# Second norm of a hybrid decoder layer: weight product formed ahead of the row factor, residual added in one operation per half

## Chip, cores, metric

The kernel runs on one core of a Trainium2 chip. The metric is the device time of one execution in microseconds; the times given are medians over runs. A profile is one execution taken by the hardware profiler; its times count from the start of its span.

## What is computed

One layer of a decoder trunk for 512 tokens of width 1024, in float32. The input is normalised and projected; eight heads of block-sparse attention and four heads of a matrix memory make the two halves of `mixed`; then come the output projection, a norm with the residual, and an MLP. The change lies between the output projection and the MLP:

```python
def rms_norm(x, g):
    y = x * lax.rsqrt(jnp.mean(x * x, axis=-1, keepdims=True) + EPS) * g
    return y

x = x + rms_norm(mixed @ w_out, g_mix_post)      # the second norm, with the residual
u = rms_norm(x, g_mlp_pre) @ w_up
u = jnp.square(jax.nn.relu(u))
x = x + rms_norm(u @ w_down, g_mlp_post)
```

## The kernel before

Each float32 operand of a matmul is split into a high and a low part, and each product is made of three matmuls (`three`). Tokens lie in four tiles of 128 (`NT`), each tile on the 128 partitions. The output projection `y = mixed @ w_out` is made in two halves of 512 columns: `yA[t]` (matmuls named ya, four PSUM banks of the pool `psm`) for all four tiles, then `yB` (matmuls named yb, one bank each of the pool `psa`, which has four) tile after tile, 24 matmuls each, six to each of four weight chunks.

Squares of `yA` with their row sums are taken on ScalarE (L785) into `s2[:, t, 0]`, and VectorE adds the epsilon (L786). Behind each tile's yb the generator `second_norm(t, yB)` is started. It takes the square of `yB` on ScalarE (L794), makes the row factor `r` from both sums with eight one-column operations on VectorE (`rsqrt`, L295 to L304), and then for each half multiplies y by r and by the weight `gpo` (L799, into a scratch tile `scr`) and adds the residual (L800), giving `x1[t]`. `gpo` is loaded at L776 from `g_post`, `x1` starts as the input x.

After its due time the generator emits, per half, four transposes of `x1` into one PSUM bank (`hTp`, L805, which the profile shows at the helper's line L218), and then four pairs that split the transposed pieces: the high part on ScalarE (L810) and the low part on VectorE (L811), both reading the same bank, into `hT`, the right-hand side of the up projection. The low part needs the high part.

Order. TensorE's instructions stand in the order in which the program writes them; those of the other engines are ordered by the builder's scheduler, by program order and by the priorities given with `high_priority`. The class `Flow` decides where a generator's matmuls go into TensorE's order: each matmul adds a booked time (columns/2.4 + 2.5 ns, a transpose 109 ns), `poll` is called after every six yb matmuls or every three up matmuls, and a generator goes on at the first poll at which its delay has passed. The delay counts from the first poll that sees the request. For the first half of a tile it is `DLY["norm"]`, for the second `DLY["nrm2"]` (256). A booked time sets the order only; on the chip TensorE waits for what its next instruction needs.

Then three up units (`EARLY`) run over the columns of tiles 0 and 1 (256 columns a matmul) once tile 1 is through the planner, and over those of tiles 2 and 3 once tile 3 is; the other up units run over 512 columns, with the first groups of the down projection among them. Up weights are split ahead by `chunk` (L197 on ScalarE, L198 on VectorE or GpSimd). The pools `ph2` and `res` lie where the tiles of the first phase lay; `pad2` and `padr` are fillers that set addresses in `ph2`. The tag "tw" of `ph2` holds the split down weights (tiles `w`) later.

Of the kernel before, what the change touches and what calls it, by code (L numbers as in the profile page):

```python
# [15 lines left out]
F32 = mybir.dt.float32  # L16
F32R = mybir.dt.float32r
# [3 lines left out]
OP = mybir.AluOpType  # L21
# [3 lines left out]
P = 128  # L25
S = 512
NT = 4
D = 1024
# [3 lines left out]

BOOST = 400
PAD2, PADR = 96, 104
DLY = {"norm": 4600, "g1": 6000, "g2": 7000, "mb": 3500, "mbh": 5640, "mav": 3325, "tp": 3000, "tph": 7150, "sta": 5320, "stb": 1250, "sh": 2200, "pt": 3500, "pth": 2200, "ao": 1500, "mo": 1900, "mix": 1550, "nrm2": 256, "hT": 1300}
WO_ORDER = (0, 1, 2, 3)
ORDERED = {mybir.EngineType.PE}
SLABS = (("mqk", 512), ("gv", 392), ("qk0", 512), ("vv", 384), ("qk1", 512), ("av1", 256), ("mo", 512))
# [69 lines left out]
def kernel(  # L108
# [17 lines left out]
    nc = tc.nc  # L126
    f = lambda ap: ap.bitcast(F32)
# [46 lines left out]
    def load_to(i):  # L174
        while state["load"] <= min(i, len(specs) - 1):
            k = state["load"]
            raws[k] = load_raw(specs[k][0], specs[k][1], f"raw{k}")
            state["load"] += 1

    def split_to(i):  # L180
        while state["split"] <= min(i, len(specs) - 1):
            k = state["split"]
            if specs[k][2] == "res" and state["res"] is None:
                return
            load_to(k)
            _, n, where = specs[k]
            if where == "ring":
                ws = ring.tile([P, 2, 1024], F32R, tag="ws", name=f"ws{k}", bufs=3)
            else:
                ws = state["res"].tile([P, 2, 1024], F32R, tag="u", name=f"ws{k}")  # L190
            raw = raws.pop(k)
            parts = 2 if k == 0 else 1
            lo = nc.gpsimd if 3 < k < n_wo and k % 2 else nc.vector
            with tc.high_priority(offset=BOOST):
                for a in range(parts):
                    sl = slice(a * n // parts, (a + 1) * n // parts)
                    nc.scalar.copy(ws[:, 0, sl], raw[:, sl])  # L197
                    lo.tensor_tensor(ws[:, 1, sl], raw[:, sl], f(ws[:, 0, sl]), op=OP.subtract)  # L198
            splits[k] = ws
            state["split"] += 1  # L200

    def chunk(i):

        split_to(i + 2)
        load_to(i + 4)
        return splits[i]
# [10 lines left out]
    def tr(o, i, idn):  # L217
        nc.tensor.transpose(o, i, idn)  # L218
        flow.pe(109.0)
# [65 lines left out]
    def rsqrt(y, s, scale, bias, tag, extra=None):  # L285


        n = s.shape[-1]
        mh = small.tile([P, n], F32, tag=tag + "m", name=tag + "m")
        g = small.tile([P, n], F32, tag=tag + "g", name=tag + "g")  # L290
        t = small.tile([P, n], F32, tag=tag + "t", name=tag + "t")
        if extra is None:
            nc.vector.tensor_scalar(mh, s, -0.5 * scale, -0.5 * bias, op0=OP.mult, op1=OP.add)
        else:
            nc.vector.tensor_scalar(mh, s, extra, -0.5 * scale, op0=OP.add, op1=OP.mult)  # L295

        nc.vector.tensor_scalar(g.bitcast(I32), mh.bitcast(I32), -0.5, 1597463007.0 - 2.0 ** 22 - 2.0 ** 30, op0=OP.mult, op1=OP.add)
        for it in range(3):
            if n == 1:
                nc.vector.scalar_tensor_tensor(t, g, mh, g, op0=OP.mult, op1=OP.mult)  # L300
            else:
                nc.vector.tensor_tensor(t, g, g, op=OP.mult)
                nc.vector.tensor_tensor(t, t, mh, op=OP.mult)
            nc.vector.scalar_tensor_tensor(y if it == 2 else g, t, 1.5, g, op0=OP.add, op1=OP.mult)  # L304
# [175 lines left out]
    def mlstm_gates():  # L480
# [16 lines left out]
        nc.vector.scalar_tensor_tensor(lf, p, -2.0, e, op0=OP.mult, op1=OP.add)  # L497
        yield dict(delay=DLY["g1"], banks=2, hold=3000)
        gi = psa.tile([P, S], F32, tag="at", name="gi")
# [36 lines left out]
        nc.vector.scalar_tensor_tensor(hm[32:36, 0:S], mx, -1.0, f(hm[0:4, 0:S]), op0=OP.mult, op1=OP.subtract)  # L536
        yield dict(delay=DLY["g2"], banks=1, hold=1500)
        ac = psa.tile([P, S], F32, tag="at", name="ac")
# [9 lines left out]
    def mlstm_head(h):  # L548
# [12 lines left out]
        for jj in ((0, 1), (2, 3)):  # L561
            yield dict(delay=DLY["mb"] if jj[0] == 0 else 0, banks=2, hold=DLY["mbh"] if jj[0] == 0 else 2000)
            for j in jj:
# [10 lines left out]
        for tt in ((0, 1), (2, 3)):  # L574
            yield dict(delay=DLY["mav"] if tt[0] == 0 else 0, banks=2, hold=1500, cond="vv" if h == 3 else None)
            for t in tt:
# [29 lines left out]
    mix = [None] * 8  # L606
# [23 lines left out]
    def att_group(g):  # L630
        qs, ks, kls = [], [], []
        for i, blk in enumerate((0, 2, 1, 3)):
            yield dict(cond=f"qk{g}" if i == 0 else None, delay=DLY["tp"] if i == 0 else 0, banks=1, hold=DLY["tph"])
            tp = psa.tile([P, S], F32, tag="at", name=f"tp{g}{blk}")
# [8 lines left out]
            if i == 1:  # L643
                yield dict(delay=DLY["sta"])
                stacks[g] = (qs, ks, kls)
# [107 lines left out]
    yA = [psm.tile([P, S], F32, tag="mm", name=f"ya{t}") for t in range(NT)]  # L753
# [14 lines left out]
    ph2 = ctx.enter_context(tc.tile_pool(name="ph2", bufs=1, reuse_waits="tile"))  # L768
# [3 lines left out]
    ph2.tile([P, PAD2], F32, name="pad2")  # L772
    x1, hT = [], ph2.tile([P, KT, 2, S], F32R, name="hT")
    scr = f(res.tile([P, 2, 1024], F32R, tag="a", name="scr", bufs=2))
    gpo, tmps = scr[:, 0], (scr[:, 1, 0:S], scr[:, 1, S:2 * S])
    nc.sync.dma_start(gpo, g_post.partition_broadcast(P))  # L776
    for t in range(NT):
        xt = ph2.tile([P, D], F32, name=f"x1_{t}")
        nc.sync.dma_start(xt, x[t])
        x1.append(xt)  # L780
    junk = ph2.tile([P, S], F32, name="junk")
    s2 = ph2.tile([P, NT, 2], F32, name="s2")
    q2 = ph2.tile([P, NT, 2], F32, name="q2")
    for t in range(NT):
        nc.scalar.activation(junk, yA[t], AF.Square, accum_out=s2[:, t, 0:1])  # L785
        nc.vector.tensor_scalar(s2[:, t, 0:1], s2[:, t, 0:1], D * EPS, None, op0=OP.add)  # L786
    wr = [chunk(i) for i in wo_chunks[1]]

    def second_norm(t, yB):

        r = small.tile([P, 1], F32, tag="r1", name="r1")
        tt = slice(t * P, (t + 1) * P)
        with tc.high_priority(offset=300):
            nc.scalar.activation(junk, yB, AF.Square, accum_out=s2[:, t, 1:2])  # L794
            rsqrt(r, s2[:, t, 1:2], 1.0 / D, None, "r1", extra=s2[:, t, 0:1])
            for half, y in ((0, yA[t]), (1, yB)):
                cc = slice(half * S, (half + 1) * S)
                tmp = tmps[half]
                nc.vector.scalar_tensor_tensor(tmp, y, r, gpo[:, cc], op0=OP.mult, op1=OP.mult)  # L799
                nc.vector.tensor_tensor(x1[t][:, cc], tmp, x1[t][:, cc], op=OP.add)  # L800
        for half in range(2):
            yield dict(delay=DLY["norm"] if half == 0 else DLY["nrm2"])
            tp = psa.tile([P, S], F32, tag="at", name="hTp")
            for k in range(4):
                tr(tp[:, k * P:(k + 1) * P], x1[t][:, half * S + k * P:half * S + (k + 1) * P], ident)  # L805
            with tc.high_priority(offset=300):
                for k in range(4):
                    kt, src = 4 * half + k, tp[:, k * P:(k + 1) * P]
                    g = gcol[:, 8 + kt:9 + kt]
                    nc.scalar.activation(hT[:, kt, 0, tt], src, AF.Copy, scale=g)  # L810
                    nc.vector.scalar_tensor_tensor(hT[:, kt, 1, tt], src, g, f(hT[:, kt, 0, tt]), op0=OP.mult, op1=OP.subtract)  # L811
        yield dict(delay=DLY["hT"])
        flow.flags.add(f"hT{t}")

    for t in range(NT):
        tt = slice(t * P, (t + 1) * P)
        yB = psa.tile([P, S], F32, tag="at", name=f"yb{t}")
# [17 lines left out]
    y = [None] * NT  # L835
# [141 lines left out]
    for t in range(NT):  # L977
        for half in range(2):
            nc.scalar.activation(junk, x1[t][:, half * S:(half + 1) * S], AF.Square, accum_out=q2[:, t, half:half + 1])
    ph2.tile([P, PADR], F32, name="padr")  # L980
    nc.vector.tensor_tensor(eps2, q2[:, :, 0], q2[:, :, 1], op=OP.add)
    nc.vector.tensor_scalar(eps2, eps2, 1.0 / D, EPS, op0=OP.mult, op1=OP.add)
    nc.vector.tensor_tensor(eps2, eps2, eps2, op=OP.mult)
# [57 lines left out]
    ygs = [f(kts.tile([P, 2, S], F32R, tag="kt", name=f"yg{t}")).rearrange("p a n -> p (a n)") for t in range(NT)]  # L1041
# [4 lines left out]
    for t in range(NT):  # L1046
# [15 lines left out]
        with tc.high_priority(offset=100):  # L1062
            r = small.tile([P, 1], F32, tag="r1", name="r1")
# [70 lines left out]
```

## Time and profile before

| | us |
|---|---|
| median of 3 runs | 595.86 (595.63 to 596.91) |
| the profiled execution | 595.46 |
| its span | 593.7 |
| TensorE matmul busy | 578.5 (97%) |
| VectorE busy | 429.4 (72%) |
| ScalarE busy | 286.4 (48%) |
| GpSimd busy | 72.6 (12%) |

Engines are named PE (TensorE, matmul), PEld (its weight load), DVE (VectorE), ACT (ScalarE), POOL (GpSimd) and SP (the DMA queue). Lines such as L811 are lines of the kernel. Matmuls are pipelined and their ends are modelled, so the distance from start to start tells more than their durations.

### The profile page before, as it was taken

The page shows a single profiled execution, that of the slowest core. Times are in us where ns is not written, and L with a number is a line of the kernel's source. Part 1 is how long each engine was busy: PE and PEld are TensorE (multiplying, and loading weights), DVE is VectorE, ACT ScalarE, POOL GpSimd, SP SyncE. Part 2 cuts the span into 40 slices and gives each one's busy share as a digit, 9 for nine tenths or more (in the row PEclk, how much of TensorE's full clock was granted, in tenths as well). Part 3 has the DMA queues.
Part 4 walks back from the last instruction along what each step waited for, and adds up shares of the span by engine and source line. Part 5 has one row for each costly group of instructions (what it writes and reads, how often), then busy time and mean ns, then how long its engine had stood idle before and what let it go on. Part 6 is the DMA issues. An engine that isn't in the chain of part 4 may idle for free.

```text
span 593.7 us, 7757 instructions
## 1 busy us (share of the span) xinstructions
PE 578.5 (97%) x2895; PEld 488.6 (82%) x2895; DVE 429.4 (72%) x790; ACT 286.4 (48%) x505; POOL 72.6 (12%) x78
## 2 busy tenths in 40 slices
PE   8999999899999999999999999999999999999995
PEld 4898898688978888898888888888888888888884
DVE  5897868687996845865778685988667986856346
ACT  5664556467756654475344344344443443444211
POOL 0133341225311040000000000000000000000132
PEclk9999999899999999999999999999999999999999
DMA  7633121102311266007611363121543114013002
GB/s 281 258 135 115 63 71 55 35 20 72 107 71 36 73 230 231 0 1 257 257 54 36 110 218 132 36 68 40 198 156 106 36 36 142 35 36 129 14 35 108
DMA packets 18470, 60.79 MB, mean 102 GB/s; under 512 B 2432, under 2 KB 2432, under 8 KB 18432
## 3 DMA queue, kind: packets, MB, share of 16 engines
q1 hardware_dynamic: 18288, 60.28, 29.3%
q8 instruction: 23, 0.38, 0.3%
q14 instruction: 15, 0.12, 0.1%
q10 hardware_dynamic: 144, 0.01, 0.0%
HBM read 58.19 MB, written 2.10 MB: 102 GB/s over the span
## 4 chain that ended last, share of the span: by engine, by line
PE 87%; DVE 8%; ACT 2%; DMA 1%; issue 1%; SPq 0%; DVEq 0%; ACTq 0%
PE up L209 29%; PE pX L209 11%; PE qk L209 7%; PE pY L209 5%; PE mo L209 4%; PE dl L209 4%; PE ya L209 4%; PE dn L209 4%; PE gv L209 3%; PE pZ L209 3%; PE mqk L209 3%; PE vv L209 2%; PE yb L209 2%; PE ao L209 1%; PE as L209 1%; PE pt L218 1%
## 5 line engine op out<-in xcount | busy, mean ns | idle before, releaser
L209 PE MATMUL up<-hT,ws 128*128 128x512 f32 (+1 forms) x840 | 180.0, 372 | 0.4 <-DVE hT L811 0.4
L209 PEld LDWEIGHTS up<-hT,ws 128*128 128x128 f32 x840 | 148.3, 188 | 27.8 <-DVE hT L811 0.6
L197 ACT CAST ws<-raw 128x1024 fp32r<-128x1024 f32 (+3 forms) x77 | 76.3, 996 | 127.6 <-PE up L209 83.7
L198 DVE TENSOR_TENSOR ws<-raw,ws 128x1024 fp32r<-128x1024 f32 (+3 forms) x61 | 73.0, 1198 | 62.2 <-ACT ws L197 61.7
L904 ACT CAST w<-b 128x1024 fp32r<-128x1024 f32 x42 | 44.3, 1055 | 61.5 <-PE pX L209 27.2
L905 DVE TENSOR_TENSOR w<-b,w 128x1024 fp32r<-128x1024 f32 x42 | 51.4, 1223 | 25.9 <-ACT w L904 25.9
L209 PE MATMUL pX<-w,a 128*128 128x512 f32 x288 | 67.2, 389 | 0.0
L209 PEld LDWEIGHTS pX<-w,a 128*128 128x128 f32 x288 | 54.1, 188 | 11.2
L198 POOL TENSOR_TENSOR ws<-raw,ws 128x1024 fp32r<-128x1024 f32 (+3 forms) x16 | 36.5, 2284 | 115.2 <-ACT ws L197 79.9
L209 PE MATMUL qk<-ws,xT 128*128 128x512 f32 x192 | 49.2, 406 | 0.0
L1043 POOL TENSOR_TENSOR yg<-y,gp 128x512 f32<-128x512 f32 x4 | 5.2, 1299 | 337.4 <-DVE y L1038 337.2
L209 PEld LDWEIGHTS qk<-ws,xT 128*128 128x128 f32 x192 | 36.0, 193 | 7.0
L209 PE MATMUL pY<-w,a 128*128 128x512 f32 x144 | 33.6, 389 | 0.0
L209 PEld LDWEIGHTS pY<-w,a 128*128 128x128 f32 x144 | 27.0, 188 | 5.6
L876 DVE TENSOR_TENSOR b<-b,b 128x1024 f32<-128x1024 f32 x24 | 29.1, 1218 | 1.4 <-DMA b<-in_w_down_dram 1.3
L209 PE MATMUL mo<-ws,xT 128*128 128x512 f32 x96 | 25.9, 407 | 0.0
L209 PE MATMUL mqk<-xT,ws 128*128 128x512 f32 x96 | 23.5, 397 | 1.4 <-ACT ws L197 0.9
L209 PEld LDWEIGHTS mqk<-xT,ws 128*128 128x128 f32 x96 | 17.6, 188 | 7.4 <-ACT ws L197 2.2
L209 PE MATMUL yb<-ws,mix 128*128 128x512 f32 x96 | 23.1, 394 | 0.0
L209 PE MATMUL ya<-ws,mix 128*128 128x512 f32 x96 | 22.9, 394 | 0.0
L676 ACT ACTIVATE pp<-as,mxs 128x128 f32<-128x128 f32 (+3 forms) x32 | 16.8, 526 | 11.0 <-DVE mxs L674 10.9
L904 ACT CAST a<-u 128x1024 fp32r<-128x1024 f32 x17 | 17.8, 1050 | 8.8 <-DVE u L846 4.9
(283 smaller groups left out, 930.9 us busy)
## 6 DMA issues: line engine op xcount, KB each, us to landing
raw<-in_w_up_dram SPq DMA_DIRECT2D x32, 512.0 KB, 3.3
b<-in_w_down_dram SPq DMA_DIRECT2D x24, 512.0 KB, 4.4
raw<-in_w_in_dram SPq DMA_DIRECT2D x15, 512.0 KB, 3.3
raw<-in_w_out_dram SPq DMA_DIRECT2D x8, 512.0 KB, 3.3
raw<-in_w_down_dram SPq DMA_DIRECT2D x8, 512.0 KB, 3.2
xs<-in_x_dram SPq DMA_DIRECT2D x4, 512.0 KB, 8.7
x<-in_x_dram SPq DMA_DIRECT2D x4, 512.0 KB, 6.6
out_dram<-yg SPq DMA_DIRECT2D x8, 256.0 KB, 2.0
```

What stands on the lines that cost most here:

```text
L197: nc.scalar.copy(ws[:, 0, sl], raw[:, sl])
L198: lo.tensor_tensor(ws[:, 1, sl], raw[:, sl], f(ws[:, 0, sl]), op=OP.subtract)
L209: nc.tensor.matmul(o, lh, rh, start=first, stop=last, skip_group_check=go_on)
L218: nc.tensor.transpose(o, i, idn)
L676: nc.scalar.activation(po, sp[:, 0:n], AF.Exp, bias=mxs[:, i:i + 1], accum_out=rs[:, i:i + 1])
L876: nc.vector.tensor_tensor(o, a, b, op=op)
L904: nc.scalar.copy(o[:, 0], src)
L905: nc.vector.tensor_tensor(o[:, 1], src, f(o[:, 0]), op=OP.subtract)
L1043: nc.gpsimd.tensor_tensor(ygs[t][:, A], y[t][:, A], gp2[:, A], op=OP.mult)
```

## The change

The weight product `ygs[t] = y * g_post` is formed without r: for half A directly behind the square of `yA`, for half B directly behind the square of `yB`, both by VectorE out of PSUM into new tiles `ygp` (tag "tw" of `ph2`). Behind r there is one operation per half, `x1 = ygs * r + x1`. `DLY["norm"]` goes from 4600 to 3300. The scratch halves `tmps` are dropped, and the filler `padr` moves ahead of the new tiles and grows by 24 columns.

```diff
-DLY = {"norm": 4600, "g1": 6000, ...
+DLY = {"norm": 3300, "g1": 6000, ...
...
-    gpo, tmps = scr[:, 0], (scr[:, 1, 0:S], scr[:, 1, S:2 * S])
+    gpo = scr[:, 0]
...
     junk = ph2.tile([P, S], F32, name="junk")
+
+    ph2.tile([P, PADR + 24], F32, name="padr")
+    ygp = [f(ph2.tile([P, 2, 1024], F32R, tag="tw", name=f"ygp{i}", bufs=2)) for i in range(2)]
+    ygs = [ygp[t // 2][:, t % 2] for t in range(NT)]
     s2 = ph2.tile([P, NT, 2], F32, name="s2")
...
     for t in range(NT):
         nc.scalar.activation(junk, yA[t], AF.Square, accum_out=s2[:, t, 0:1])
         nc.vector.tensor_scalar(s2[:, t, 0:1], s2[:, t, 0:1], D * EPS, None, op0=OP.add)
+        nc.vector.tensor_tensor(ygs[t][:, 0:S], yA[t], gpo[:, 0:S], op=OP.mult)
...
             nc.scalar.activation(junk, yB, AF.Square, accum_out=s2[:, t, 1:2])
+            nc.vector.tensor_tensor(ygs[t][:, S:D], yB, gpo[:, S:D], op=OP.mult)
             rsqrt(r, s2[:, t, 1:2], 1.0 / D, None, "r1", extra=s2[:, t, 0:1])
-            for half, y in ((0, yA[t]), (1, yB)):
+            for half in range(2):
                 cc = slice(half * S, (half + 1) * S)
-                tmp = tmps[half]
-                nc.vector.scalar_tensor_tensor(tmp, y, r, gpo[:, cc], op0=OP.mult, op1=OP.mult)
-                nc.vector.tensor_tensor(x1[t][:, cc], tmp, x1[t][:, cc], op=OP.add)
+                nc.vector.scalar_tensor_tensor(x1[t][:, cc], ygs[t][:, cc], r, x1[t][:, cc], op0=OP.mult, op1=OP.add)
...
-    ph2.tile([P, PADR], F32, name="padr")
```

## Rows read from the trace of the kernel before

**Rows 1.** The page: busy time of TensorE, share of the span, instructions.

```profile
PE 578.5 (97%) x2895; PEld 488.6 (82%) x2895; DVE 429.4 (72%) x790; ACT 286.4 (48%) x505; POOL 72.6 (12%) x78
```

**Rows 2.** The chain that ended last: start us, us, what and how many.

```profile
206.25 1.22 PE ao L209 x8
...
258.81 44.54 PE up L209 x243
303.36 5.44 PE pX L209 x24
```

**Rows 3.** Waits, 198 to 266: us in total, times, longest.

```profile
ACT hT L810 <- DVE hT L811: 6.2, 9, 2.1
```

**Rows 4.** Timeline of TensorE: start, us, instruction, count, idle before and its releaser.

```profile
226.39 12.41 PE L209 MATMUL yb<-ws,mix 128*128 128x512 f32 x54
...
245.03 0.60 PE L218 MATMUL hTp<-cs,x 128*128 128x128 f32 x4
...
250.06 0.52 PE L209 MATMUL up<-hT,ws 128*128 128x256 f32 x3
...
250.77 0.60 PE L209 MATMUL up<-hT,ws 128*128 128x256 f32 x3
251.75 0.66 PE L218 MATMUL hTp<-cs,x 128*128 128x128 f32 x4 [0.38 <-DVE hT L811]
252.17 2.30 PE L209 MATMUL up<-hT,ws 128*128 128x256 f32 x16
254.91 2.66 PE L209 MATMUL up<-hT,ws 128*128 128x256 f32 x20 [0.44 <-DVE hT L811]
257.41 0.60 PE L218 MATMUL hTp<-cs,x 128*128 128x128 f32 x4
...
258.57 7.68 PE L209 MATMUL up<-hT,ws 128*128 128x256 f32 x62
```

**Rows 5.** Stretches: length, busy us of each engine, granted clock, DMA share, GB/s.

```profile
237.00:250.00 13.00, 13.00 (x66) 10.77 (x66) 10.96 (x36) 5.06 (x16) 0.00 (x0) 1.00 0.00 0
250.00:258.60 8.60, 7.78 (x63) 7.25 (x62) 6.95 (x25) 8.47 (x29) 0.00 (x0) 1.00 0.01 2
```

**Rows 6.** Timeline of VectorE, tile 0 (the same for each tile).

```profile
232.81 0.21 DVE L295 TENSOR_SCALAR r1m<-s 128x1 f32<-128x1 f32 x1 [1.73 <-ACT junk L794]
...
234.60 0.75 DVE L799 SCALAR_TENSOR_TENSOR scr<-ya,r,scr 128x512 f32<-128x512 f32 x1
235.27 0.74 DVE L799 SCALAR_TENSOR_TENSOR scr<-yb,r,scr 128x512 f32<-128x512 f32 x1
235.93 1.28 DVE L800 TENSOR_TENSOR x<-scr,x 128x512 f32<-128x512 f32 x2
```

**Rows 7.** Timeline of VectorE, tile 3, with the first of the L811 between.

```profile
251.04 0.21 DVE L295 TENSOR_SCALAR r1m<-s 128x1 f32<-128x1 f32 x1 [0.37 <-ACT junk L794]
...
251.36 0.60 DVE L811 SCALAR_TENSOR_TENSOR hT<-hTp,gcol,hT 128x128 fp32r<-128x128 f32 x2
...
254.78 0.68 DVE L800 TENSOR_TENSOR x<-scr,x 128x512 f32<-128x512 f32 x1
```

**Rows 8.** Groups by line on VectorE, tail: busy us, mean ns of one.

```profile
L1066 DVE SCALAR_TENSOR_TENSOR yg<-yg,r,x 128x512 f32<-128x512 f32 x8 | 5.7, 746 | 0.2
L1038 DVE TENSOR_TENSOR y<-dn,y 128x512 f32<-128x512 f32 x4 | 2.8, 691 | 8.9 <-PE dn L209 8.9
```

**Rows 9.** Timeline at 44 us: two engines read one PSUM bank.

```profile
44.08 0.23 DVE L455 SCALAR_TENSOR_TENSOR gts<-gv,rstd,gb 128x8 f32<-128x8 f32 x1 [0.16 <-PE gv L209]
...
44.34 0.58 ACT L451 ACTIVATE mv<-gv,rstd 128x384 fp32r<-128x384 f32 x1 [0.23 <-DVE gts L455]
```

**Rows 10.** Timeline of the DMA queue: the load of the weight `gpo`.

```profile
207.51 0.33 SPq L776 DMA_DIRECT2D scr<-in_g_post_dram  x1
```

**Rows 11.** DMA issues: engine, operation, count, KB, median us to landing.

```profile
scr<-in_g_post_dram SPq DMA_DIRECT2D x1, 512.0 KB, 4.1
```

**Rows 12.** Timeline of VectorE, first of three splits of up weights.

```profile
226.82 1.22 DVE L198 TENSOR_TENSOR ws<-raw,ws 128x1024 fp32r<-128x1024 f32 x1 [2.01 <-ACT ws L197]
```

More of the change, by code (lines that the diff above doesn't have):

```diff
@@ L34 @@
 PAD2, PADR = 96, 104
-DLY = {"norm": 4600, "g1": 6000, "g2": 7000, "mb": 3500, "mbh": 5640, "mav": 3325, "tp": 3000, "tph": 7150, "sta": 5320, "stb": 1250, "sh": 2200, "pt": 3500, "pth": 2200, "ao": 1500, "mo": 1900, "mix": 1550, "nrm2": 256, "hT": 1300}
+DLY = {"norm": 3300, "g1": 6000, "g2": 7000, "mb": 3500, "mbh": 5640, "mav": 3325, "tp": 3000, "tph": 7150, "sta": 5320, "stb": 1250, "sh": 2200, "pt": 3500, "pth": 2200, "ao": 1500, "mo": 1900, "mix": 1550, "nrm2": 256, "hT": 1300}
 WO_ORDER = (0, 1, 2, 3)
```

## Prediction

> **What bounds the kernel now.** I read the page first: TensorE is busy for 578.5 of 593.7 us [rows 1]. The chain of waits says the same more sharply: from the up projection on it is TensorE and nothing else [rows 2]. So only two things can move the time: time in which TensorE stands in the stretch that the change touches, and the tail, which it does not touch. The stretch runs from the second half of the output projection (yb) to the first up matmuls, 226 to 259 us. TensorE's clock is granted at 1.00, the 2.4 GHz level, in all of it [rows 5], so clock is no term.
>
> How much does TensorE lose there? The pace is known. The chain has 243 up matmuls in 44.54 us; 144 of them have 512 columns, at 5.44/24 = 0.2267 us, so the 99 with 256 columns take (44.54 - 32.64)/99 = 0.120 us [rows 2]. A group of four transposes hTp costs 0.40 us, from (1.16 - 3 x 0.12)/2 between 257.41 and 258.57, or 0.48, from (23.67 - 96 x 0.2267)/4 between 226.39 and 250.06, where four groups stand among the 96 yb matmuls; I take 0.44 [rows 4]. Between 250.06 and 258.57 TensorE runs 45 up matmuls and four groups: 5.40 + 1.76 = 7.16 of 8.51 us. **It loses 1.35 us** (1.2 to 1.5 by the two group costs). The idle figures of the rows, 0.38 and 0.44, say less, because the modelled ends of matmuls cover part of each stall. Start to start, the first stall is 251.75 - (250.77 + 0.08 + 3 x 0.12) = 0.54, the second 254.91 - (252.17 + 0.08 + 16 x 0.12) = 0.74, where 0.08 is the extra step behind a transpose (0.44 - 0.36); refilling makes the rest. In the yb part none of the four groups carries a wait, as the one at 245.03 shows [rows 4]. From 258.57 on TensorE runs at its pace. So **1.35 us, 0.23%, is all that this change can win**.
>
> Both stalls end with VectorE's L811, which writes the low part of hT: one frees a PSUM bank for the transposes of tile 2, the other delivers the last piece of tile 1. VectorE is the tight engine: 10.96 of 13.0 us busy between 237 and 250 [rows 5].
>
> **The change, part by part.** *Behind r.* In tile 0, which nothing disturbs, the square lands at 232.81, the eight small operations of r take 1.79 us, and the four wide ones (two L799, two L800) 2.61 us, to 237.21 [rows 6]. Afterwards two remain, of the form of L1066 in the tail: 0.746 us, two in a row 0.75 + 0.66 = 1.41 [rows 8]. The product of yB, PSUM times SBUF, has the form of L1038: 0.691, in a queue about 0.61 (L799 follows L799 after 0.67 of its 0.75) [rows 6, 8].
>
> *Does that product run beside the square?* The trace says no. Where both engines read one PSUM bank, the second waits: gts on VectorE reads gv from 44.08 to 44.31, and mv on ScalarE, which reads other columns and needs nothing of gts, begins at 44.34, released by it [rows 9]. Likewise ScalarE's hT waits nine times, 6.2 us, for VectorE's L811 of the piece before, in the same bank [rows 3]. The square is written first, so the product waits for it and stands ahead of r, on VectorE. Chain per tile: 0.61 + 1.79 + 1.41 = 3.81 in place of 4.40, so 0.59 us saved, not the 1.2 of two operations. First half of x1: 3.15 in place of 3.79. VectorE is relieved by the same 0.59 per tile.
>
> The Trainium skill ("PSUM — Partial Sum Buffer", section "PSUM bank collisions raise a hardware error") speaks against the change here: two engines must not touch one bank and quadrant at once, two reads included, and software has to order them. The order of gts and mv agrees. By it the chain saves 0.59 us per tile; without it 1.2.
>
> *The product of yA* moves to before yb, four times 0.69 = 2.8 us of VectorE. Between 223 and 232 VectorE does three splits of some 1.22 us and four small sums, and waits for ScalarE between them, 2.01 us before the first split [rows 12]. The products come behind the squares of ya for the bank's sake. The splits that they may push back belong to up weights, first needed at 250.06: some 20 us of cover. SP's weight loads, which wait for these splits, slip by 2.8 us at most; the next split weights are used after the first three up units, past 266. Without that cover the 2.8 us would be paid. The weight gpo is issued at 207.51 and lands after 4.1 us [rows 10, 11], 11 us before the first square of ya. The new tiles ygp lie where the w tiles of the down projection go much later; ph1's tiles under them were last read by the attention matmuls, which end at 207.5 [rows 2]. The moved pad keeps w in place, by my count of the bytes, and shifts res by 96. I cost that at nothing; a wait there would show at the squares of ya. Since yA and yb are read early, their banks come free before r; nothing waits on that except possibly hTp, in the change's favour.
>
> *The due time, 4600 to 3300 ns.* The planner books 1.295 us for six yb matmuls, and the delay runs from the first poll after the tile: 1.295 + 4.6 is met at the fifth poll (30 matmuls), 1.295 + 3.3 at the fourth (24). The 54 matmuls ahead of the first hTp agree (24 of tile 0, then 30) [rows 4]. So the transposes of tiles 0 and 1 go ahead six matmuls earlier, 1.36 us; those of tile 2 right behind yb, three up matmuls earlier; those of tile 3 after 36 up matmuls in place of 42, 0.72 us. The count of TensorE's work stays.
>
> *What is late next.* TensorE runs in order, so x1 of each tile must be there by its transposes. Tile 0: x1's first half at 232.81 + 3.15 = 235.96, transposes at 226.39 + 48 x 0.2267 = 237.27: 1.3 us spare. The square lands 232.81 - (226.39 + 24 x 0.2267) = 0.98 behind the tile's last yb. Tile 1: 237.27 + 0.98 + 3.15 = 241.4, plus the L811 slipped in. In tile 3 seven of them stand between 251.04 and the end of L800 at 255.46, of which 1.79 + 1.35 is the chain: 0.18 each [rows 7]. With eight: 242.8, transposes at 243.6 (24 yb matmuls and two groups, 0.88, later). Tile 2 the same: 243.6 + 0.98 + 3.15 + 1.44 = 249.2 against 250.06. Tile 3 is tight: transposes at 250.06 + 36 x 0.12 + 2 x 0.44 = 255.26; x1 at 251.04 + 3.15 = 254.19 plus L811, with four 254.9, with seven 255.46. So **a new stall of 0 to 0.3 us**, and as much again if the second half is late. The two old stalls: the transposes of tile 1 come 1.4 us earlier (243.6, not 245.03) and VectorE has shed 1.2 us by 250 (tiles 1 and 2), together more than the 0.54 and 0.74 by which they were late. I take them as gone.
>
> Sum on the profiled execution, 595.46 us (span 593.7 and 1.8 around it): -1.35 + 0.3 = -1.05, so 594.4. That execution lies 0.4 below the median of the runs; on the median, 595.86 - 1.05 = **594.8 us**. Bounds of the sum: -1.5 to +0.3 with tile 3 late by 1.65.
>
> **The rivals.** *A, all of the loss goes.* Tile 3 gets its x1 in time, because few L811 are left by 251. For it: the relief of VectorE. Against: the eight L811 of tile 2 fall due in just that chain. 595.86 - 1.35 = 594.5. A product that does run beside the square, 0.6 sooner, would end here too.
>
> *B, the stall moves.* VectorE's order is set by the builder, not by the due time, and earlier transposes bring more L811 into the chains of tiles 1 and 2. One old stall stays and the new one comes: -1.35 + 0.74 + 0.3 = -0.3, so 595.6.
>
> *C, slower.* The order puts all L811 that are left at yb's end ahead of tile 3's chain: four of tile 1 and eight of tile 2 at 0.34 unoverlapped, 4.1 us. Then x1 comes at 251.04 + 3.15 + 4.1 = 258.3, and TensorE stands 3.0 us before the transposes of tile 3: 595.86 - 1.35 + 3.0 = 597.5. It turns into a loss above 0.2% when the first half of x1 of tile 3 ends after 255.26 + 1.35 + 1.19 = 257.8. Against it: r's small operations have been slotted between L811, not behind them [rows 7].
>
> **How the numbers follow.** What a measurement of this kernel can tell from no change is about 0.2%, 1.19 us, so 594.67 is the border, close to my number. Chances: forecast 0.45, A 0.33, B 0.14, C 0.08. The forecast's own spread (594.4 to 595.2) puts a little of it under the border and nearly all of A lies there, so faster 0.39, same 0.53, slower 0.08. Range 594.2 to 596.0: A less 0.3 us for the spread of medians, up to B with 0.4 us; beyond it remain C and 0.05 at the low end.
>
> **What would show it.** Right: the two stalls at 251.75 and 254.91 gone, hTp's first group after 48 yb matmuls, the yB product beginning after the square's end on VectorE, r about 0.6 later behind the square than before, two wide operations behind r in 1.41 us, first pX unit near 302.3. A wait of hTp on x1 at tile 3 is the new stall. Wrong: product and square overlapping in time, a wait at yb or at the splits before 232 us, or up matmuls slower than 0.120 us.

## The result, and the profile after

The changed kernel is slower: 598.77 us (597.47 to 600.92) against 595.51 us (593.33 to 597.62) for the kernel before, a ratio of 1.0058 with a 95% interval of 1.0048 to 1.0069, so 2.9 to 4.1 us. The forecast was 594.8. Its profiled execution took 598.34 us, with a span of 596.6.

In the second norm nearly everything came as forecast. This is the timeline of TensorE in the changed kernel (start, us, instruction, count); no row carries a wait in brackets, where [rows 4] had two.

```profile
225.16 11.37 PE L209 MATMUL yb<-ws,mix 128*128 128x512 f32 x48
236.37 0.60 PE L218 MATMUL hTp<-cs,x 128*128 128x128 f32 x4
...
249.30 0.60 PE L218 MATMUL hTp<-cs,x 128*128 128x128 f32 x4
249.65 0.61 PE L209 MATMUL up<-hT,ws 128*128 128x256 f32 x3
250.10 0.60 PE L218 MATMUL hTp<-cs,x 128*128 128x128 f32 x4
250.46 4.19 PE L209 MATMUL up<-hT,ws 128*128 128x256 f32 x33
254.48 0.65 PE L218 MATMUL hTp<-cs,x 128*128 128x128 f32 x4
254.88 0.60 PE L209 MATMUL up<-hT,ws 128*128 128x256 f32 x3
255.40 0.66 PE L218 MATMUL hTp<-cs,x 128*128 128x128 f32 x4
255.81 14.45 PE L209 MATMUL up<-hT,ws 128*128 128x256 f32 x112
```

The first transposes stand after 48 yb matmuls, those of tile 3 after 36 up matmuls, and between 249.30 and 255.81 TensorE runs four groups and 39 up matmuls in 6.51 us, of which 4 x 0.44 + 39 x 0.120 = 6.44 is work.

The loss is elsewhere. The chain that ended last (start us, us, what and how many), changed kernel; pX, pY and pZ are units of the down projection, dn and dl its last part:

```profile
225.32 11.21 PE yb L209 x48
...
301.31 5.61 PE pX L209 x24
306.92 5.47 PE up L209 x24
312.39 5.61 PE pZ L209 x24
...
544.87 22.13 PE dn L209 x96
567.00 22.44 PE dl L209 x120
```

and the rows of the kernel before that answer to the last two ([rows 2] has its pX unit, 5.44):

```profile
542.72 21.76 PE dn L209 x96
564.48 22.08 PE dl L209 x120
```

Matmuls of the same shape, at the same granted clock, have become slower: 24 of a down unit take 5.61 us in place of 5.44, 233.8 ns each in place of 226.7, though the chain shows no wait there. The sum from the first yb on: up to the first pX unit 301.31 - 225.16 = 76.15 in place of 303.36 - 226.39 = 76.97, so -0.82; from there to the end of the span 295.29 in place of 290.34, so +4.95, of which the 21 down units are 3.6 (0.17 each), dn 0.37, dl 0.36 and the up units between them (5.47 for 5.44) about 0.6. Net +4.1. That the spans differ by 2.9 only is the stage ahead: the first yb comes 1.2 us earlier in this execution. The granted clock accounts for it: in the kernel before it was 0.50, the 1.2 GHz level, between 110.0 and 113.4 us, behind a wait of TensorE of 2.57 us, and twelve qk matmuls took 4.29 us there; in the changed kernel it stayed at 1.00 behind a wait of 2.58 us, and the same twelve took 2.83. The change does not touch that stage, and in the profiles shown here it ends anywhere between 224.1 and 227.7; stretches are therefore compared from the first yb on.

### The profile page after: what moved, and what is told of

It is laid out like the page before. It is cut to its first block, busy times and chain, and to the rows that moved or that the text cites. A ratio compares the mean times of both kernels' runs of the same rounds, so it can differ in the third digit from the quotient of the medians.

```text
span 596.6 us, 7757 instructions
## 1 busy us (share of the span) xinstructions
PE 581.8 (98%) x2895; PEld 487.6 (82%) x2895; DVE 429.1 (72%) x790; ACT 286.5 (48%) x505; POOL 72.6 (12%) x78
## 4 chain that ended last, share of the span: by engine, by line
PE 90%; DVE 6%; ACT 1%; DMA 1%; issue 1%; SPq 0%; DVEq 0%; ACTq 0%
PE up L209 29%; PE pX L209 11%; PE qk L209 7%; PE pY L209 6%; PE mo L209 4%; PE dl L209 4%; PE yb L209 4%; PE dn L209 4%; PE ya L209 4%; PE gv L209 3%; PE pZ L209 3%; PE mqk L209 3%; PE vv L209 2%; PE ao L209 1%; PE as L209 1%; PE pt L218 1%
## 5 line engine op out<-in xcount | busy, mean ns | idle before, releaser
L209 PE MATMUL pX<-w,a 128*128 128x512 f32 x288 | 69.3, 396 | 0.0
L209 PE MATMUL qk<-ws,xT 128*128 128x512 f32 x192 | 47.8, 397 | 0.0
```

What stands on the lines that cost most here:

```text
L209: nc.tensor.matmul(o, lh, rh, start=first, stop=last, skip_group_check=go_on)
```

## Theories

Theory A, addresses: the change moves the tiles of the pool `res` (by 96 bytes, as the prediction counted, at no cost), and matmuls with an operand in them became slower. Rival S: the new order of work, or VectorE's new operations, slow TensorE. A matmul has two operands in SBUF: the stationary one, which the weight load (PEld) brings in, and the moving one, whose columns follow. The bytes at which they begin, in each partition, as the built programs give them, and the remainder by 256, called the offset here:

```
tile                          before   mod 256   changed   mod 256
ws, mix, y (ring, kts)         33696       160     33696       160
hT                            110240       160    110240       160
w (ph2, down weights)         161952       160    161952       160
a (res)                       178336       160    178432         0
u, ws of w_out, second half   194720       160    194816         0
```

In the kernel before every operand of these stages begins at the offset 160 within 256 bytes; that is what its fillers of 96 and 104 columns brought about. In the changed kernel the three small tiles s2, q2 and eps2 lie behind w, and the filler ahead of w grew by their 96 bytes: w stayed, and everything in `res` went to the offset 0.

The changed kernel's trace holds a comparison of its own. The 96 dn matmuls have one shape and the same moving operand (ws, offset 160), but half take the stationary one from `a` (now at 0) and half from `hT` (still at 160). Groups on TensorE (busy us, mean ns of one):

```profile
L209 PE MATMUL dn<-ws,a 128*128 128x512 f32 x48 | 11.4, 396 | 0.0
L209 PE MATMUL dn<-ws,hT 128*128 128x512 f32 x48 | 11.0, 389 | 0.0
```

Start to start they take 234.2 and 226.7 ns; in the kernel before, 226.6 and 226.7.

## Experiments

**The changed kernel at the old addresses.** The small tiles go back ahead of the filler, and the filler to its old size.

```diff
+    s2 = ph2.tile([P, NT, 2], F32, name="s2")
+    q2 = ph2.tile([P, NT, 2], F32, name="q2")
+    eps2 = ph2.tile([P, NT], F32, name="eps2")
-    ph2.tile([P, PADR + 24], F32, name="padr")
+    ph2.tile([P, PADR], F32, name="padr")
     ygp = [...]
-    s2 = ph2.tile([P, NT, 2], F32, name="s2")
-    q2 = ph2.tile([P, NT, 2], F32, name="q2")
...
-    eps2 = ph2.tile([P, NT], F32, name="eps2")
```

> The changed kernel with s2, q2 and eps2 allocated ahead of the filler and the filler at its old 104 columns, so that the w tiles and every tile of the pool res lie at the addresses that they have before the change. Nothing else differs from the changed kernel. Theory A (addresses): matmuls with an operand in res went from 226.7 to about 234 ns because res moved by 96 bytes; here yb, pX, pY, pZ, dn and dl go back to 226.7 ns and only the gain of the second norm remains: 595.5 - 1.35 = 594.2 us. Rival S (the new order of work, or the new VectorE work, slows TensorE): pace stays at 234 ns and the time near 598.8 us.

Measured: 594.10 us against 595.24, ratio 0.9979 (0.9967 to 0.9990). Its chain, and the first rows of its TensorE timeline:

```profile
303.23 5.44 PE pX L209 x24
308.67 5.44 PE up L209 x24
...
542.59 21.76 PE dn L209 x96
564.35 22.08 PE dl L209 x120
```

```profile
227.56 11.05 PE L209 MATMUL yb<-ws,mix 128*128 128x512 f32 x48
```

The pace is back in every unit, and from the first yb to the first pX it takes 303.23 - 227.56 = 75.67 us, 1.30 less than before. The whole slow-down was the addresses, and the change itself wins about what the prediction gave as all that it could win.

**The kernel before, with `res` moved.** One unused tile behind w, no instruction changed.

```diff
+    ph2.tile([P, 24], F32, name="padz")
     gp2 = f(kts.tile(...
```

> The kernel before with one unused tile of 96 bytes allocated behind the w tiles, so that only the pool res moves by 96 bytes; no instruction changes. Theory A: yb +0.5, the 21 down units of pX, pY, pZ +0.17 each, the up units some 0.03 each, dn and dl +0.36 each, in all about +5: 600 to 601 us, that is slower than the changed kernel by the 1.35 that the norm wins there. Rival S: 595.5 us, pace 226.7 ns.

Measured: 600.42 us, ratio 1.0085 (1.0068 to 1.0103). In its chain:

```profile
304.06 5.61 PE pX L209 x24
309.68 5.47 PE up L209 x24
...
547.62 22.13 PE dn L209 x96
569.75 22.44 PE dl L209 x120
```

The same slow units, with not one instruction of the change. Rival S has fallen.

**The kernel before, with w and `res` moved together.**

```diff
-    ph2.tile([P, PADR], F32, name="padr")
+    ph2.tile([P, PADR + 24], F32, name="padr")
```

> The kernel before with its filler 24 columns wider, so that the w tiles and the pool res both move by 96 bytes; no instruction changes. If a pair of operands at different offsets within 256 bytes is what is slow (A1), pX, pY and pZ, whose operands w and a move together, keep 226.7 ns, while yb, dn and dl, with one operand moved, run at about 234: some +1.3, 596.8 us. If an operand that begins at a multiple of 256 is slow by itself (A2), pX, pY and pZ are slow as well: 600 to 601 us. Rival S: 595.5 us.

Measured: 599.14 us, ratio 1.0072 (1.0059 to 1.0085).

```profile
303.86 5.50 PE pX L209 x24
309.35 5.48 PE up L209 x24
...
545.32 22.13 PE dn L209 x96
567.44 22.44 PE dl L209 x120
```

Between the two forecasts, and the unit shows why. With both operands at 0 a pX unit takes 5.50. Start to start, its first nine matmuls take 236, 233, 236, 224, 231, 236, 228, 233 and 231 ns and the others 226 or 227, up to the last; the up units between, whose operands both lie at 160, begin much the same. So a pair with equal offsets reaches the full pace, at 0 as at 160, and a pair with unequal ones (dn's with `a`, 234.2 ns) does not; behind a change from pairs at one offset to pairs at the other it takes about nine matmuls to get there. The changed kernel shows the same: where twelve dl matmuls with both operands in `res` (both at 0) follow others, their steps are 235, 234, 236, 224, 231, 235, 229, 232, 231, 227, 226. A1 holds, but its 596.8 us left out these slow starts, some 2.1 us. In the trace the stretch from the first yb on is 3.3 us longer than before; the times differ by 3.5 to 5.1, so some tenths stay unexplained.

**The changed kernel with `res` 256 bytes beyond its old place.**

```diff
     eps2 = ph2.tile([P, NT], F32, name="eps2")
+    ph2.tile([P, 40], F32, name="padz")
```

> The changed kernel with an unused tile of 160 bytes behind eps2, so that res lies 256 bytes beyond its place in the kernel before: another address, the same offset within 256 bytes. If the offset within 256 bytes (or within a divisor of it) decides, pace 226.7 ns and 594.2 us. If what lies under or beside the tiles decides, or the new order of work does, 598.8 us.

Measured: 594.06 us, ratio 0.9974 (0.9963 to 0.9985); 5.44 us in a pX unit, 21.76 in dn. Another address with the same offset is as good as the old one, so what lies under or beside the tiles is not the cause.

**Other distances: `res` moved by 128, 64 and 32 bytes** from the old addresses, by an unused tile of 32, 16 and 8 columns behind w.

> The changed kernel at the old addresses with the pool res moved by 128 bytes. Operands in res then differ from the others by 128 within 256 bytes, and agree with them within 128 and within 64. If agreement within 128 bytes (or 64) is enough, pX runs at 226.7 ns per matmul and the time is 594.1 us; if it takes 256, at about 234 ns and 599 us.

> The changed kernel at the old addresses with the pool res moved by 64 bytes: it agrees with the other operands within 64 bytes, not within 128. If agreement within 64 bytes is enough, pX runs at 226.7 ns and the time is 594.1 us; else at about 234 ns and 599 us.

> The changed kernel at the old addresses with the pool res moved by 32 bytes. 64, 96 and 128 bytes were slow (233 to 234 ns in pX); if any difference within 256 bytes is, this is slow as well: 232 to 234 ns and 598 to 599 us; if an operand that begins within the same 64 bytes is read as before, 226.7 ns and 594.1 us.

Measured: 599.0, 597.6 and 597.3 us, one execution each; in the last two the first yb came 1.1 and 1.4 us earlier than in the kernel before, so the units tell more than the times. Chains, in this order:

```profile
302.85 5.59 PE pX L209 x24
...
545.71 22.05 PE dn L209 x96
567.75 22.35 PE dl L209 x120
```

```profile
301.17 5.60 PE pX L209 x24
...
544.45 22.11 PE dn L209 x96
566.56 22.05 PE dl L209 x120
```

```profile
301.14 5.59 PE pX L209 x24
...
544.00 22.09 PE dn L209 x96
566.09 22.27 PE dl L209 x120
```

All three are slow in pX and dn (233 ns a matmul), so it takes agreement within 256 bytes, not within 128, 64 or 32. One exception is seen, where the moving operand is the one that lies apart, by 64 bytes: yb loses only 0.12 in its first 48 matmuls (11.01 in place of 10.89, where the other distances lose 0.30 to 0.32), and dl as a whole nothing (22.05). In dl two things cancel: start to start, its 512-column matmuls with `hT` take 229.2 ns in place of 226.6, and its 256-column ones 113.4 in place of 120.0. At 96 bytes, in the changed kernel, the 256-column ones with `hT` take 119.7 and those of 512 columns 233.6: only the latter are slowed. Why 64 bytes differs there is open.

**The products alone, and the due time alone**, both at the old addresses: the changed kernel with `DLY["norm"]` at 4600, and the kernel before with it at 3300.

> The changed kernel at the old addresses with the due time of the norm put back from 3300 to 4600: the products without the earlier transposes. If the relief of VectorE (0.59 us per tile) is what ends the two stalls before the up projection, both are gone here too, or all but 0.2 us, and the time is that of the changed kernel at the old addresses, 594.1 to 594.4 us. If the earlier transposes did it, one or both stalls stay (0.74 us or 1.35 us): 594.9 to 595.4 us. VectorE's relief of 1.2 us by the third tile is as much as the stalls, so the first is likelier.

> The kernel before with the due time of the norm at 3300 alone: four wide operations behind r as before. If the earlier transposes are what wins, the stalls are gone: 594.1 us. If VectorE's work is the bound, its queue is as long as before while the transposes are asked for earlier: the stall moves to the transposes of tile 3 (x1 there at about 255.4 us of the trace before, asked for at 255.26, second half 1.5 us later), so 0.3 to 1.6 us are lost again: 594.5 to 595.8 us.

Measured: the products alone 593.58 us against 594.30, ratio 0.9982 (0.9963 to 1.0002); the due time alone 596.34 us, ratio 1.0032 (1.0015 to 1.0049). The times alone do not tell the first from no change; the rows do. TensorE's timeline with the products alone:

```profile
227.67 12.41 PE L209 MATMUL yb<-ws,mix 128*128 128x512 f32 x54
...
252.04 0.60 PE L209 MATMUL up<-hT,ws 128*128 128x256 f32 x3
252.48 0.60 PE L218 MATMUL hTp<-cs,x 128*128 128x128 f32 x4
252.84 4.55 PE L209 MATMUL up<-hT,ws 128*128 128x256 f32 x36
```

Both stalls of [rows 4] are gone with the transposes at their old places; to the first pX unit (303.46) it takes 75.79 us, 1.18 less than before. With the due time alone:

```profile
226.35 11.05 PE L209 MATMUL yb<-ws,mix 128*128 128x512 f32 x48
...
246.11 0.66 PE L218 MATMUL hTp<-cs,x 128*128 128x128 f32 x4 [0.51 <-DVE hT L811]
...
256.60 0.66 PE L218 MATMUL hTp<-cs,x 128*128 128x128 f32 x4 [0.54 <-DVE x L800]
257.01 0.60 PE L209 MATMUL up<-hT,ws 128*128 128x256 f32 x3
258.12 0.66 PE L218 MATMUL hTp<-cs,x 128*128 128x128 f32 x4 [0.51 <-DVE x L800]
```

The stall moves, as expected, to the transposes of tile 3, which now wait for L800, and one comes at tile 1; to the first pX unit (304.03) it takes 77.68 us, 0.71 more than before, somewhat worse than the bound given. So VectorE's relief is the gain, and in these traces the due time adds 0.12 us to it; without the relief it costs.

**All operands of the attention stage at the same offset too.**

```diff
+    const.tile([P, 32], F32, name="padc")
     cs = const.tile([P, C_W], F32, name="cs")
...
+    const.tile([P, 32], F32, name="padd")
     gb = const.tile([P, 8], F32, name="gb")
...
+    one.tile([P, 40], F32, name="pade")
     identb = one.tile([P, P], BF16, name="identb")
...
+    one.tile([P, 32], F32, name="padf")
     num = one.tile([P, NT, 4, P], F32, name="num")
```

> The changed kernel at the old addresses, and unused tiles that bring the identity matrices, the mask, the selector and the tile num of the attention stage to the offset 160 within 256 bytes that the other operands have (they lay at 32, 0 and 128). If a change of offset between successive operands is what costs TensorE some nanoseconds, the matmuls that follow transposes and mask products get faster: qk from about 230 to 227 ns (192 of them, 0.6 us), mo from 231.4 to 227 (96, 0.4 us), yb and ya by a little: 0.5 to 1.2 us less than the changed kernel at the old addresses, 593.0 to 593.6 us. If it is something about the pool res alone, nothing changes: 594.1 us.

Measured: 593.94 us, ratio 0.9981 (0.9969 to 0.9993), the same as at the old addresses. Groups of the page on TensorE (busy us, mean ns of one), this kernel:

```profile
L209 PE MATMUL qk<-ws,xT 128*128 128x512 f32 x192 | 47.7, 396 | 0.0
L209 PE MATMUL mo<-ws,xT 128*128 128x512 f32 x96 | 25.9, 407 | 0.0
```

mo is what it was, to the nanosecond, and start to start qk and mo stay at 229 and 231 ns. (qk's mean was 406 in the kernel before, because of the stretch at a granted clock of 0.50; here the clock was 1.00.) What slows them is not the offset of the tiles that were moved: a miss. The steps in the trace show where the time goes. A series of 36 qk matmuls in the kernel before, at 54.72 us, has, behind its first, the steps 235, 233, 236, 224, 231, 235, 229, 232 and 231 ns and then 225 to 228 up to its last. That is the slow start of the pX units above, here behind matmuls of other shapes. mo stands mostly in series of six between transposes and mask products, and such a series ends before the pace is reached. So a series starts slowly behind matmuls of other shapes too; why is open.

## Why the prediction was wrong

*The bound.* The prediction put the possible gain at 1.35 us, by TensorE's loss between 250.06 and 258.57. At equal addresses the change wins 1.30 us in that stretch, and 0.21% (0.10 to 0.33) of the time. Right; and since little was lost again at tile 3 (below), the stretch went rather as rival A had it.

*Product and square in one bank.* Right, step by step. VectorE in the changed kernel, tile 0:

```profile
231.75 0.69 DVE L800 TENSOR_TENSOR ygp<-yb,scr 128x512 f32<-128x512 f32 x1 [2.34 <-ACT junk L799]
232.36 0.20 DVE L295 TENSOR_SCALAR r1m<-s 128x1 f32<-128x1 f32 x1
...
234.14 1.42 DVE L804 SCALAR_TENSOR_TENSOR x<-ygp,r,x 128x512 f32<-128x512 f32 x2
```

The product is released by the square, of which it needs nothing, and stands ahead of r; the chain is 0.61 + 1.78 + 1.42 = 3.81 us, as worked out, for 4.40 in [rows 6]. It does not run beside the square. The section of the Trainium skill that the prediction weighed ("PSUM — Partial Sum Buffer", section "PSUM bank collisions raise a hardware error") agrees with this row: the two reads are kept apart.

*Which stalls go.* Both, as forecast, and through VectorE's relief, as the products alone show. The new stall at tile 3 was put at 0 to 0.3 us; TensorE's starts there are 0.05 (first half) and 0.13 us (second half) late.

*The failed step.* "The moved pad keeps w in place, by my count of the bytes, and shifts res by 96. I cost that at nothing", and with it the sentence that from 258.57 on TensorE runs at its pace. The count was right. The price was +5.4 us in the traces: +4.95 from the first pX on, and 0.48 in yb (76.15 in the changed kernel up to the first pX, 75.67 at the old addresses); by the medians it was 4.7 (598.77 against 594.10). The prediction looked for the cost of an address in waits on what lay there before and for nothing else. The sign that it named for slower matmuls, up matmuls above 0.120 us, did not come: these kept 0.120, and the slow ones were yb and the down projection, to which it gave no price, no chance and so no part of the range.

Could the rows have warned? Matmuls of one shape did not all have one pace in the kernel before: two of its groups on the page,

```profile
L209 PE MATMUL pX<-w,a 128*128 128x512 f32 x288 | 67.2, 389 | 0.0
L209 PE MATMUL mo<-ws,xT 128*128 128x512 f32 x96 | 25.9, 407 | 0.0
```

differ by 18 ns in the mean duration, and start to start by 4.7 (231.4 against 226.7). The matmuls that read a tile in `res` are 96 of yb, 504 of the down units, 48 of dn and 120 of dl: 768, and at 4.7 ns each 3.6 us. Taken as a bound, at even a small chance, that would have stretched the range to 598.4 us. But it would have come near by luck: mo is slow because its series are short, while its own operands both lie at 160. The real warning stood in the code: two fillers whose sizes set addresses, and a change that alters one of them.

*The rivals.* C had a loss, for another reason: the first half of x1 of tile 3 ended 29.3 us behind the first yb (at 254.4), and C becomes a loss only at 31.4 (257.8 - 226.39). That its 597.5 lies nearest to the measured time is luck.

## What to carry to other kernels

An unused tile is a part of a change like any other. When a change adds, drops or reorders tiles in a pool, write down at which offset each matmul operand begins before and after, and keep the two operands of a matmul at equal offsets; here that is 0.8 to 0.9% of the time, about four times what the edited stage had to give. And when a term is put at "nothing", look for what would show it otherwise: a filler that does no work is there for some reason, and a kernel with nothing but a filler changed, as above, shows its price. Of the edit itself, the part that paid was taking work off the engine that others waited for, not asking for its result sooner.

The version to keep is the changed kernel at the old addresses, or with `res` 256 bytes further: 594.1 us, ahead of both kernels.

## What the runs showed of the hardware

In a series of float32r matmuls of 128 by 128 and 512 columns, one starts every 226.7 ns when the stationary and the moving operand begin at equal offsets within 256 bytes of a partition (both at 160, or both at 0), and every 232 to 234 ns when the offsets differ by 32, 64, 96 or 128 bytes, whichever of the two lies apart (but 229 where the moving one lies apart by 64). The 256-column ones of dl lost nothing (119.7 ns at a difference of 96 bytes, 120.0 at none). Such a series often starts slowly: up to nine steps of 224 to 236 ns before the pace is reached, seen behind pairs at another offset and behind transposes and matmuls of other shapes. The granted clock was 1.00 in these stretches of either kernel that were read, so it is not the clock. What in the reading of operands does this was not tried.
